# Expert inputs of a mixture-of-experts layer: selection matmuls replaced by rows gathered from DRAM

## The chip, the cores and the metric

The kernel runs on one core of one Trainium2 chip. The metric is the device time of one execution in microseconds, as the median of several runs. Traces come from one further execution under the hardware profiler.

## What is computed

One decoder layer on x of 512 tokens x 1024 features, float32. First three attention mixers in parallel, gated, projected and added; then a layer norm; then a mixture of experts with a second layer norm. The change lies in the mixture of experts:

```
x = layer_norm(ALPHA * x + mix)                    # x1: 512 x 1024
g = top-1 of 4 groups (softmax probability g_p)
two experts = top-2 of the 8 experts of that group
gate = g_p * softmax(the two logits)               # one weight per token and expert
for each expert e of 32, on the rows xb of x1 that chose it:
    h = silu(xb @ w_gate[e]) * (xb @ w_up[e])      # 1024 -> 512
    y = h @ w_down[e]                              # 512 -> 1024
out = layer_norm(ALPHA * x1 + sum over its two experts of gate * y)
```

There are 512 x 2 = 1024 assignments of a token to an expert. Each expert has three weight matrices of 2 MiB in float32, 192 MiB for all experts; each weight is read once.

## The kernel before

**Stages.** Up to about 411 us the attention part runs, with its weights streamed by SP through a pool of its own. From 411 to 450 us the last four blocks of the output projection are added to x1 tile by tile (project, in the order of the string ORDER, line 47), each tile of 128 tokens is normalised (norm, line 595), transposed (turn_x), routed (route) and ranked within its expert (rank). Then come 16 steps of two experts each, from 451 us on, and the second layer norm.

**Slots.** Each expert has 64 slots, so a pair of experts fills one tile of 128 rows. An assignment whose rank in its expert is 64 or more is left to an overflow loop (line 1138), which handles one expert with 64 further rows per iteration; how many iterations there are is known only on the chip (overflow_table, line 901, called in step 1; the count is read into a register of every engine at line 1137). The loop stands between step 7 and step 8 (MIDP = 7).

**One step** (pair_step, line 1016), in the order of TensorE, which is written out by hand: up(p, 0), the gate matrix, 16 matmuls of 64 slots x 512 columns, two experts side by side; the products of the step before are put back to token order and added to x1 for two token tiles (combine, line 789); up(p, 1), the up matrix; hidden (Silu on ScalarE, product on VectorE); combine of the other two tiles; selection for later pairs; turn (four transposes of the hidden rows, copied out as hT); info (per slot: its gate and its token number); down(p, 0) and down(p, 1). VectorE, ScalarE, GpSimd (Pool) and SP are ordered by the compiler's scheduler, each engine works its queue in order.

**Expert inputs.** An expert needs its rows of x1 transposed, 1024 features over partitions and slots in columns (xg). Before, this is a product with a 0/1 matrix: VectorE compares the slot numbers with each token's place (select; Quad.start, line 819, for two pairs at once, 256 columns), and TensorE multiplies x1 by it. Pair 0 does this while routing runs (gather0, line 870), pair 1 in float32 in step 0 (gather, line 744), and the pairs 2 to 15 by twos from a high and a low float32r half of x1 (split2 and Quad.gather, lines 808 and 828), 32 matmuls of 256 columns in a step, in steps 1 to 13. The two halves fill the tile xb, 32 KB a partition.

**Weights.** A weight matrix is fetched by SP in two pieces of 128 partitions x 2048 (1 MiB each, fetch, line 527). Pieces go round through 13 ring slots (RB, RA, RC, RD = 4, 5, 3, 1; lines 516 to 525); the tile xb holds four pieces before it is needed for x1's halves, and a tile named once holds two for step 0. A piece is issued when its slot's last reader on TensorE is done. ahead(n) (line 554) issues the next n pieces of the list; once the list of those fetched is used up, weights (line 540) issues one where it is asked for. Before the overflow loop as many pieces as the ring holds, less two, are issued (line 1133):

```
1130      with tc.manual_schedule(engines={mybir.EngineType.PE}):
1131          pairs[0].info()
1132          steps(range(MIDP + 1))
1133      ahead(RA + RB + RC + RD - 2)
```

At the loop's entry all engines meet, and SP waits until its DMAs have landed.

Of the kernel before, what the change touches and what calls it, by code (L numbers as in the profile page):

```python
# [22 lines left out]
P = 128  # L23
S = 512
# [12 lines left out]
RA, RB, RC, RD = 5, 4, 3, 1  # L37
HALF = 2048
MIDP = 7
# [11 lines left out]
def layer(ctx, tc, xT, xn, memT, w_qk, w_v, w_mk, w_mv, w_g, w_o, rb, oh, ln, wr, br,  # L51
# [562 lines left out]
    xbp = ctx.enter_context(pool("xb", waits="tile"))  # L614
# [6 lines left out]
    t = xbp.tile([P, 4 * HALF], F32, name="xb", tag="xb")  # L621
    ahead(4, [t[:, i * HALF:(i + 1) * HALF] for i in range(4)])
# [5 lines left out]
    i256 = rpool.tile([P, 256], F32, name="i256")  # L628
    ve.tensor_copy(i256[:, 0:P], i128)
    ve.tensor_scalar(out=i256[:, P:2 * P], in0=i128, scalar1=float(P), scalar2=None, op0=ALU.add)  # L630
# [90 lines left out]
    class Pair:  # L721
# [4 lines left out]
        def start(self):  # L726
            if self.p < 2:
                self.sel = gpool2.tile([P, TT, P], F32, name="sel", tag="sel", bufs=2)
                self.xg = (gpool2.tile([P, KT, P], F32, name="xg0", tag="xg0", bufs=1) if self.p == 0 else
                           quadp[0].tile([P, KT, 2 * P], F32, name="xg", tag="xg", bufs=2)[:, :, 0:P])  # L730
            else:
                self.sel = gpool2.tile([P, 2 * TT, P], BF16, name="sel", tag="sel", bufs=2)[:, 0:TT, :]
                self.xg = quads[self.p // 2].xg[:, :, self.p % 2 * P:self.p % 2 * P + P]
# [10 lines left out]
        def gather(self, c, bank="xgp"):  # L744
# [8 lines left out]
        def info(self):  # L753
            sp = bank3("ht" if self.p == 0 else "xgp")
            for t in range(TT):
                if self.p < 2:
                    pe.matmul(sp[:, 0:3], self.sel[:, t, :], gmx[:, t, self.p, :], start=t == 0, stop=t == TT - 1)
                else:
                    for i in range(3):
                        pe.matmul(sp[:, 0:3], self.sel[:, t, :], gmb[0][:, i, t, self.p, :], start=t + i == 0,  # L760
                                  stop=t + i == TT + 1)
            si = ep.tile([P, 8], F32, name="si", tag="si", bufs=3)
            ve.tensor_copy(si[:, 0:3], sp[:, 0:3])
            ve.tensor_copy(si[H[1], 0:1], sp[H[1], 1:2])
            self.si = si
# [40 lines left out]
    xb = [None]  # L806

    def split2(c):

        r = slice(c * 512, (c + 1) * 512)  # L810
        for t in range(TT):
            split(xb[0][:, 0, t, r], xb[0][:, 1, t, r], x1[:, t, r])

    class Quad:

        def __init__(self, m):
            self.m = m

        def start(self):
            self.sel = quadp[0].tile([P, TT, 2 * P], F32R, name="selq", tag="selq", bufs=1)  # L820
            self.xg = quadp[0].tile([P, KT, 2 * P], F32, name="xg", tag="xg", bufs=2)
            for t in range(TT):
                d = [d0[:, t, j, 2 * self.m:2 * self.m + 1] for j in range(2)]
                ve.tensor_scalar(out=self.sel[:, t, :], in0=i256, scalar1=d[0], scalar2=None, op0=ALU.is_equal)
                ve.scalar_tensor_tensor(out=self.sel[:, t, :], in0=i256, scalar=d[1], in1=self.sel[:, t, :].bitcast(F32),
                                        op0=ALU.is_equal, op1=ALU.add)

        def gather(self, i, bank):
            o = bank3(bank)
            for j in range(2):  # L830
                k = 2 * i + j
                for t in range(TT):
                    for part in range(2):
                        pe.matmul(o[:, j * 256:(j + 1) * 256], xb[0][:, part, t, k * P:(k + 1) * P], self.sel[:, t, :],  # L834
                                  start=t + part == 0, stop=t + part == TT)
            sc.copy(self.xg[:, 2 * i:2 * i + 2, :], o.rearrange("p (k t) -> p k t", t=256))  # L836

    quadp, quads = [], [Quad(m) for m in range(8)]

    def split_gates():  # L840
        gmb[0] = g = late[0].tile([P, 3, TT, 16, 3], BF16, name="gmb")
        f = lambda a: a.rearrange("p t a c -> p (t a c)")
        r = late[0].tile([P, TT * 48], F32, name="gr", tag="sq", bufs=1)
        ve.tensor_copy(f(g[:, 0]), f(gmx))
        ve.tensor_tensor(out=r, in0=f(gmx), in1=f(g[:, 0]), op=ALU.subtract)
        ve.tensor_copy(f(g[:, 1]), r)
        ve.tensor_tensor(out=f(g[:, 2]), in0=r, in1=f(g[:, 1]), op=ALU.subtract)
# [434 lines left out]
```

## Time and profile before

| | us |
|---|---|
| median of 3 runs | 961.93 |
| lowest, highest | 961.65, 962.98 |
| the profiled execution | 960.1 |
| its span, first to last instruction | 958.3 |

The page of the profile gives each engine's busy time in the span and, in 40 equal slices of 24 us, its busy share and what the DMA moved. The chain of waits follows the work that ended last back in time. A stretch is a window between two times of the span, with each engine's busy time, the granted clock of TensorE (1.00 is 2.4 GHz, 0.50 is 1.2 GHz), the share of the 16 DMA engines in use and GB/s. A timeline lists instructions in order; a DMA there is its issue, and its landing is told by its tile's view. PE is TensorE, PEld its weight load, DVE VectorE, ACT ScalarE, POOL GpSimd, SP the engine that issues most DMAs; a q behind an engine is its sequencer.

### The profile page before, as it was taken

How to read it: one execution, taken by the hardware profiler on the slowest of the kernel's cores; microseconds unless marked ns; L12 is line 12 of the kernel's file. 1: busy time of each engine (PE TensorE's matmuls, PEld its weight loads, DVE VectorE, ACT ScalarE, POOL GpSimd, SP SyncE). 2: the span in 40 equal slices, each digit the busy share in tenths (PEclk: the TensorE clock that was granted, in tenths of full speed). 3: DMA queues.
4: the chain of work that ended last, by engine and by line, in shares of the span. 5: the costliest groups of instructions: out<-in, count | busy, mean ns of one | idle time of the engine just before them, and what ended most of it. 6: DMA issues, size and time to landing. Idle time of an engine off the chain costs nothing.

```text
span 958.3 us, 12603 instructions
## 1 busy us (share of the span) xinstructions
PE 916.2 (96%) x4924; PEld 592.1 (62%) x4924; DVE 483.1 (50%) x1084; ACT 267.1 (28%) x505; POOL 30.7 (3%) x24
## 2 busy tenths in 40 slices
PE   7999999999999999999999999999879999999992
PEld 6888888787788888877554455445425455344430
DVE  5686776566764443478445353332234433332337
ACT  6365555456222222323131110011101111011013
POOL 2000000000000000310000000000000000000003
PEclk9999999999999999999999999999979999999997
DMA  8242231222344523378498999999989999999942
GB/s 301 75 134 89 93 118 63 82 73 67 134 178 140 197 88 102 101 313 346 176 369 334 415 421 421 420 419 421 420 319 374 421 420 421 421 421 420 420 180 88
DMA packets 44213, 249.52 MB, mean 260 GB/s; under 512 B 5713, under 2 KB 6904, under 8 KB 19704
## 3 DMA queue, kind: packets, MB, share of 16 engines
q1 hardware_dynamic: 42480, 247.84, 65.3%
q10 hardware_dynamic: 1672, 0.85, 0.4%
q8 instruction: 40, 0.66, 0.3%
q14 instruction: 21, 0.17, 0.1%
HBM read 246.57 MB, written 2.11 MB: 259 GB/s over the span
## 4 chain that ended last, share of the span: by engine, by line
PE 91%; DVE 5%; DMA 2%; ACT 1%; issue 1%; SPq 0%; POOL 0%; DVEq 0%; ACTq 0%; POOLq 0%
PE gu L982 23%; PE dn L1009 11%; PE pj L124 9%; PE pj L126 9%; PE pj L125 9%; PE xgp L834 3%; PE cb L834 3%; PE cb L798 2%; PE z L126 2%; PE z L124 2%; PE z L125 2%; PE y L278 2%; PE cb L799 2%; PE dn L798 1%; PE dn L799 1%; PE z L267 1%
## 5 line engine op out<-in xcount | busy, mean ns | idle before, releaser
L982 PE MATMUL gu<-r,xg 128*64 128x512 f32 x992 | 221.6, 600 | 8.8 <-DMA r<-in_we_dram 8.8
L982 PEld LDWEIGHTS gu<-r,xg 128*64 128x64 f32 x992 | 70.4, 138 | 148.3 <-issue 145.5
L103 DVE TENSOR_TENSOR wl<-wraw,wh 128x1024 fp32r<-128x1024 f32 (+2 forms) x71 | 82.3, 1162 | 86.1 <-ACT wh L102 85.7
L124 PE MATMUL pj<-xh,wh 128*128 128x512 f32 x304 | 120.7, 397 | 0.0
L125 PE MATMUL pj<-xh,wl 128*128 128x512 f32 x304 | 118.7, 390 | 1.1 <-DVE wl L103 1.1
L126 PE MATMUL pj<-xl,wh 128*128 128x512 f32 x304 | 118.9, 391 | 0.0
L1009 PE MATMUL dn<-r,hT 128*64 128x512 f32 x496 | 111.0, 596 | 1.2 <-ACT hT L999 1.2
L102 ACT CAST wh<-wraw 128x1024 fp32r<-128x1024 f32 (+2 forms) x71 | 70.3, 990 | 78.5 <-PE z L126 23.5
L801 DVE TENSOR_TENSOR x<-x,cb 128x512 f32<-128x512 f32 x60 | 38.4, 681 | 82.9 <-PE cb L799 78.6
L1009 PEld LDWEIGHTS dn<-r,hT 128*64 128x64 f32 x496 | 34.6, 137 | 64.3 <-issue 61.1
L124 PEld LDWEIGHTS pj<-xh,wh 128*128 128x128 f32 x304 | 57.1, 188 | 14.2 <-issue 2.0
L125 PEld LDWEIGHTS pj<-xh,wl 128*128 128x128 f32 x304 | 57.2, 188 | 12.7 <-DVE wl L103 1.4
L126 PEld LDWEIGHTS pj<-xl,wh 128*128 128x128 f32 x304 | 57.1, 188 | 12.0
L991 DVE SCALAR_TENSOR_TENSOR u<-gu,si,g 128x512 f32<-128x512 f32 x16 | 12.0, 750 | 99.1 <-PE gu L982 81.1
L836 ACT COPY xg<-xgp 128x512 f32<-128x512 f32 x14 | 8.2, 586 | 162.2 <-PE xgp L834 162.2
L103 DVE TENSOR_TENSOR y_l<-dn,y_h 128x512 fp32r<-128x512 f32 x31 | 21.4, 691 | 63.5 <-ACT y_h L102 63.3
L102 ACT CAST y_h<-dn 128x512 fp32r<-128x512 f32 x31 | 18.1, 585 | 94.5 <-PE dn L1009 94.5
L990 ACT ACTIVATE g<-gu 128x512 f32<-128x512 f32 x16 | 9.6, 598 | 108.6 <-PE gu L982 108.6
L385 ACT ACTIVATE gt<-pj 128x512 f32<-128x512 f32 x24 | 14.3, 598 | 89.9 <-PE pj L126 89.9
L801 DVE TENSOR_TENSOR x<-x,dn 128x512 f32<-128x512 f32 x60 | 38.3, 679 | 0.0
L834 PE MATMUL cb<-selq,xb 128*128 128x256 f32 x224 | 29.9, 286 | 0.0
L834 PEld LDWEIGHTS xgp<-selq,xb 128*128 128x128 f32 x224 | 28.6, 191 | 1.1
(626 smaller groups left out, 1390.0 us busy)
## 6 DMA issues: line engine op xcount, KB each, us to landing
r<-in_we_dram SPq DMA_DIRECT2D x185, 1024.0 KB, 11.5
wraw<-in_w_g_dram SPq DMA_DIRECT2D x32, 512.0 KB, 3.4
wraw<-in_w_qk_dram SPq DMA_DIRECT2D x14, 512.0 KB, 3.5
wraw<-in_w_v_dram SPq DMA_DIRECT2D x16, 384.0 KB, 3.5
wraw<-in_w_o_dram SPq DMA_DIRECT2D x8, 512.0 KB, 3.4
xb<-in_we_dram SPq DMA_DIRECT2D x4, 1024.0 KB, 7.1
xraw<-in_xT_dram SPq DMA_DIRECT2D x4, 512.0 KB, 6.4
x<-in_xn_dram SPq DMA_DIRECT2D x4, 512.0 KB, 5.5
```

The costliest lines, as they stand in the source:

```text
L102: sc.copy(dst_h, src)
L103: (gp if eng is gp else ve).tensor_tensor(out=dst_l, in0=src, in1=dst_h.bitcast(F32), op=ALU.subtract)
L124: pe.matmul(o, lh, rh, start=start and i == 0, stop=False)
L125: pe.matmul(o, ll, rh, start=False, stop=False)
L126: pe.matmul(o, lh, rl, start=False, stop=stop and i == n - 1)
L278: pe.matmul(ycur[0][H[a], i * P:(i + 1) * P], self.v[:, j, self.vcol + a * 64:self.vcol + a * 64 + 64], self.pT[a][:, j * P:(j + 1) * P], ...
L798: pe.matmul(o, sT, self.y_h[c][0:n], start=True, stop=False)
L799: pe.matmul(o, sT, self.y_l[c][0:n], start=False, stop=True)
L801: ve.tensor_tensor(out=x1[:, t, r], in0=x1[:, t, r], in1=o, op=ALU.add)
L834: pe.matmul(o[:, j * 256:(j + 1) * 256], xb[0][:, part, t, k * P:(k + 1) * P], self.sel[:, t, :], start=t + part == 0, stop=t + part == TT)
L982: pe.matmul(o[H[q]], pairs[p].xg[:, k, H[q]], held[q][:, k % 4 * 512:k % 4 * 512 + 512], start=k == 0, stop=k == KT - 1)
L1009: pe.matmul(o[H[q]], hT[:, k, H[q]], w[q][:, k * 512:(k + 1) * 512], start=k == 0, stop=k == 3)
```

## The change

Each tile of x1 is also stored to a DRAM tile xdr (512 x 1024) when it is normalised, by a DMA issued from Pool. For the pairs 1 to 15 the selection matmuls are gone, and with them Quad, xb, its split and the 256-column comparisons. Instead the slot information of pair p + 2 (its token numbers) is computed in step p between the two down products, turned into row numbers (rows), and Pool issues an indirect DMA that fetches up to 128 rows of 4 KB from xdr into one tile xrow; row numbers outside 0 to 511 (empty slots) are left out. In step p + 1, behind the combine, eight transposes make xg of it (spread). There is one xrow and one xg tile. Pair 1's information and rows are issued in step 0 behind up(0, 0). The information matmuls of a pair take the three bfloat16 parts of the gates in one product of nine columns, where there were three products. The freed space makes ring1 nine slots and ring3 four: 18 for 13. The overflow loop moves from behind step 7 to behind step 0 (overflow_table from step 1 to step 0), with six pieces issued ahead of it. The scaling of x1 by ALPHA moves from the end of step 0 to behind up(0, 0). The loop's body fetches its rows in the same way.

```diff
-RA, RB, RC, RD = 5, 4, 3, 1
+RA, RB, RC, RD = 9, 4, 4, 1
-MIDP = 7
+MIDP = 0
+BEFORE = 6
-    t = xbp.tile([P, 4 * HALF], F32, name="xb", tag="xb")
-    ahead(4, [t[:, i * HALF:(i + 1) * HALF] for i in range(4)])
     ahead(RA)
...
+        def info(self, bank="xgp"):
+            sp = bank3(bank)
+            si = ep.tile([P, 8], F32, name="si", tag="si", bufs=3)
+            if self.p < 2:
+                for t in range(TT):
+                    pe.matmul(sp[:, 0:3], self.sel[:, t, :], gmx[:, t, self.p, :], start=t == 0, stop=t == TT - 1)
+                ve.tensor_copy(si[:, 0:3], sp[:, 0:3])
+            else:
+                for t in range(TT):
+                    pe.matmul(sp[:, 0:9], self.sel[:, t, :], gmb[0][:, t * 16 + self.p, :], start=t == 0, stop=t == TT - 1)
+                ve.tensor_reduce(out=si[:, 0:3], in_=sp[:, 0:9].rearrange("p (i c) -> p c i", c=3), axis=AX.X, op=ALU.add)
...
+        def rows(self, n=P):
+
+            ix = ep.tile([P, 1], I32, name="ix", tag="ix", bufs=2)
+            ve.tensor_scalar(out=self.si[0:n, 3:4], in0=self.si[0:n, 2:3], scalar1=0.5, scalar2=BIG, op0=ALU.is_lt, op1=ALU.mult)
+            ve.scalar_tensor_tensor(out=ix[0:n], in0=self.si[0:n, 2:3], scalar=-1.0, in1=self.si[0:n, 3:4], op0=ALU.add, op1=ALU.add)
+            gp.indirect_dma_start(xrow[0][0:n], None, xdr, bass.IndirectOffsetOnAxis(ap=ix[0:n, 0:1], axis=0),
+                                  bounds_check=S - 1, oob_is_err=False)
+
+        def spread(self, c, bank):
+
             o = bank3(bank)
+            if c == 0:
+                self.xg = gpool2.tile([P, KT, P], F32, name="xg", tag="xg", bufs=1)
             for j in range(4):
                 k = 4 * c + j
-                srcs = [(x1[:, t, k * P:(k + 1) * P], self.sel[:, t, :]) for t in range(TT)]
-                for i, (a, b) in enumerate(srcs):
-                    pe.matmul(o[:, j * P:(j + 1) * P], a, b, start=i == 0, stop=i == len(srcs) - 1)
+                pe.transpose(o[:, j * P:(j + 1) * P], xrow[0][:, k * P:(k + 1) * P], ident)
             sc.copy(self.xg[:, 4 * c:4 * c + 4, :], o.rearrange("p (k t) -> p k t", t=P))
...
         if 1 in cols:
             norm(t, sm, lnb, op)
+            gp.dma_start(xdr[ts, :], x1[:, t, :])
...
-    quadp.append(ctx.enter_context(pool("quad", waits="tile")))
+    xrow[0] = ctx.enter_context(pool("rowp", waits="tile")).tile([P, D], F32, name="xrow")
+    gp.memset(xrow[0], 0.0)
...
         g = up(p, 0)
+        if p == 0:
+            pairs[1].info("cb")
+            pairs[1].rows()
+            pairs[0].info("ht")
+            for t in range(TT):
+                sc.mul(x1[:, t, :], x1[:, t, :], ALPHA)
...
-        for i, (of, u) in enumerate(units):
-            if i == n:
-                hT = turn(hs)
-            of.gather(u, ("xgp", "cb")[i % 2])
-        if p >= 14:
-            hT = turn(hs)
-        if p < 15:
-            pairs[p + 1].info()
-        for c in range(2):
-            down(p, hT, c)
+        if p < 15:
+            pairs[p + 1].spread(0, "xgp")
+        hT = turn(hs)
+        if p < 15:
+            pairs[p + 1].spread(1, "cb")
         if p == 0:
-            xb[0] = xbp.tile([P, 2, TT, D], F32R, name="xb", tag="xb")
-            split2(0)
-            split2(1)
-            for t in range(TT):
-                sc.mul(x1[:, t, :], x1[:, t, :], ALPHA)
-        if p == 1:
             overflow_table()
+        down(p, hT, 0)
+        if p < 14 and p != MIDP:
+            pairs[p + 2].info()
+            pairs[p + 2].rows()
+        down(p, hT, 1)
...
-            if p == 1 or p in range(2, 14, 2):
-                quads[p // 2 + 1].start()
-            if p + 1 < 16:
-                choose(p + 1)
+            if p + 2 < 16:
+                choose(p + 2)
             pair_step(p)
 
     with tc.manual_schedule(engines={mybir.EngineType.PE}):
-        pairs[0].info()
+        choose(1)
         steps(range(MIDP + 1))
-    ahead(RA + RB + RC + RD - 2)
+    ahead(BEFORE)
...
     with tc.manual_schedule(engines={mybir.EngineType.PE}):
         pairs[MIDP].places()
+        pairs[MIDP + 2].info()
+        pairs[MIDP + 2].rows()
         steps(range(MIDP + 1, 16))
```

## Rows read from the trace of the kernel before

**Rows 1.** The page: busy us (share of the span), and GB/s in 40 slices.
```profile
PE 916.2 (96%) x4924; PEld 592.1 (62%) x4924; DVE 483.1 (50%) x1084; ACT 267.1 (28%) x505; POOL 30.7 (3%) x24
GB/s 301 75 134 89 93 118 63 82 73 67 134 178 140 197 88 102 101 313 346 176 369 334 415 421 421 420 419 421 420 319 374 421 420 421 421 421 420 420 180 88
```

**Rows 2.** TensorE's waits, 440 to 960 us: total, times, longest, in us.
```profile
PE gu L982 <- DMA r<-in_we_dram: 8.8, 1, 8.8
```

**Rows 3.** The chain that ended last: start us, us, what.
```profile
602.82 6.87 PE gu L982 x32
...
622.68 0.44 PE ht L997 x4
...
632.34 6.87 PE gu L982 x32
...
880.24 6.87 PE gu L982 x32
...
906.46 6.87 PE gu L982 x32
```

**Rows 4.** Stretches: length, busy us by engine, clock, DMA share, GB/s.
```profile
448.00:456.00 8.00, 8.00 (x51) 4.62 (x51) 7.26 (x33) 1.17 (x2) 0.00 (x0) 1.00 0.56 169
466.00:482.00 16.00, 16.00 (x108) 10.30 (x109) 11.00 (x51) 6.57 (x13) 0.00 (x0) 1.00 0.07 14
506.00:512.00 6.00, 6.00 (x43) 2.52 (x43) 5.36 (x20) 1.17 (x2) 0.00 (x0) 1.00 0.32 97
696.00:732.00 36.00, 31.77 (x160) 14.82 (x162) 16.00 (x47) 2.84 (x5) 0.00 (x0) 0.87 0.83 320
```

**Rows 5.** The chain that ended last, at the overflow loop.
```profile
688.43 10.89 DMA r<-in_we_dram
```

**Rows 6.** Line 1138, the loop: durations ns, first and last start us.
```profile
L1138 PEldq EVENT_SEMAPHORE  x9: 51/51/51, 691.5 to 699.9; - x9
L1138 POOLq EVENT_SEMAPHORE  x8: 42/43/43, 694.4 to 699.8; - x8
```

**Rows 7.** A stretch of the loop; columns as in group 4.
```profile
696.00:700.00 4.00, 0.00 (x0) 0.00 (x0) 0.00 (x0) 0.00 (x0) 0.00 (x0) 0.50 0.34 135
```

**Rows 8.** A stretch at the kernel's start; columns PE, PEld, DVE, ACT, POOL.
```profile
10.00:20.00 10.00, 10.00 (x79) 10.00 (x79) 6.67 (x6) 7.31 (x11) 2.52 (x1) 1.00 1.02 384
```

**Rows 9.** The tile r, weight pieces: first and last start us; issue to landing.
```profile
L982 PE MATMUL gu<-r,xg x992: 592/593/1116, 450.9 to 921.8; 128*64 128x512 f32 x199
...
DMA to landing us min/median/max: 5.0/11.6/21.1
```

**Rows 10.** Timeline of SP, 411 to 467 us: first issue, length, pieces.
```profile
411.82 2.06 SPq L533 DMA_DIRECT2D xb<-in_we_dram  x4
413.92 21.54 SPq L533 DMA_DIRECT2D r<-in_we_dram  x8
440.52 0.80 SPq L533 DMA_DIRECT2D once<-in_we_dram  x2
450.06 8.79 SPq L533 DMA_DIRECT2D r<-in_we_dram  x5
```

**Rows 11.** Timeline of TensorE in step 0: start us, us, what.
```profile
464.82 3.84 PE L750 MATMUL xgp<-sel,x 128*128 128x128 f32 x32
...
476.88 3.60 PE L1009 MATMUL dn<-r,hT 128*64 128x512 f32 x16
```

**Rows 12.** Timeline of VectorE: the overflow table, from expert counts to iteration count.
```profile
514.09 0.19 DVE L912 COPY ov<-ht 128x32 f32<-128x32 f32 x1 [1.90 <-PE ht L910]
...
518.90 0.16 DVE L924 CAST ovi<-ove 1x17 int32<-1x17 f32 x1
```

**Rows 13.** Timeline of SP, 900 to 910 us: the last weight pieces.
```profile
903.05 4.24 SPq L533 DMA_DIRECT2D r<-in_we_dram  x4
```

**Rows 14.** DMA issues by size: KB each, median us to landing (the last two half pieces).
```profile
r<-in_we_dram SPq DMA_DIRECT2D x2, 512.0 KB, 12.4
```

**Rows 15.** Timeline of TensorE: the last down product.
```profile
931.31 3.65 PE L1009 MATMUL dn<-r,hT 128*64 128x512 f32 x14
```

More of the change, by code (lines that the diff above doesn't have):

```diff
@@ L613, in layer @@
     ring1 = ctx.enter_context(pool("ring1", bufs=RA, waits="tile"))
-    xbp = ctx.enter_context(pool("xb", waits="tile"))
     rpool = ctx.enter_context(pool("rout", waits="tile"))
@@ L742, in select @@
                                     op0=ALU.is_equal, op1=ALU.add)
-        def gather(self, c, bank="xgp"):
+        def info(self, bank="xgp"):
[9 more added lines that the diff above has]
+                ve.tensor_reduce(out=si[:, 0:3], in_=sp[:, 0:9].rearrange("p (i c) -> p c i", c=3), axis=AX.X, op=ALU.add)
+            ve.tensor_copy(si[H[1], 0:1], si[H[1], 1:2])
+            self.si = si
@@ L751, in gather @@
             sc.copy(self.xg[:, 4 * c:4 * c + 4, :], o.rearrange("p (k t) -> p k t", t=P))
-        def info(self):
-            sp = bank3("ht" if self.p == 0 else "xgp")
-            for t in range(TT):
[L756 to L765, printed above, removed]
@@ L804, in combine @@
                                                 op1=ALU.add, accum_out=sums[:, t, c:c + 1])
[L806 to L836, printed above, removed]
@@ L838, in layer @@
-    quadp, quads = [], [Quad(m) for m in range(8)]
-    def split_gates():
[L841 to L847, printed above, removed]
+    def split_gates():
+        gmb[0] = g = late[0].tile([P, TT * 16, 9], BF16, name="gmb")
+        f = lambda a: a.rearrange("p t a c -> p (t a) c")
+        r = late[0].tile([P, TT * 16, 3], F32, name="gr", tag="sq", bufs=1)
+        ve.tensor_copy(g[:, :, 0:3], f(gmx))
+        ve.tensor_tensor(out=r, in0=f(gmx), in1=g[:, :, 0:3], op=ALU.subtract)
+        ve.tensor_copy(g[:, :, 3:6], r)
+        ve.tensor_tensor(out=g[:, :, 6:9], in0=r, in1=g[:, :, 3:6], op=ALU.subtract)
@@ L849, in layer @@
+    xdr = ctx.enter_context(pool("xdrp", space=DRAM)).tile([S, D], F32, name="xdr")
+    xrow = [None]
     late, gmb = [None], [None]
@@ L895, in layer @@
         settle()
+    pairs[0].xg = gpool2.tile([P, KT, P], F32, name="xg", tag="xg", bufs=1)
     for c in range(2):
@@ L1030, in pair_step @@
             pairs[p - 1].combine((3,), banks=("dn", "dn"))
-        units = []
-        if p == 0:
-            units = [(pairs[1], 0), (pairs[1], 1)]
-        elif p < 14:
-            units = [(quads[p // 2 + 1], i) for i in (range(4) if p == 1 else range(2) if p % 2 == 0 else range(2, 4))]
-        n = (len(units) + 1) // 2
-        for i, (of, u) in enumerate(units):
-            if i == n:
-                hT = turn(hs)
-            of.gather(u, ("xgp", "cb")[i % 2])
-        if p >= 14:
-            hT = turn(hs)
-        if p < 15:
-            pairs[p + 1].info()
-        for c in range(2):
-            down(p, hT, c)
-        if p == 0:
-            xb[0] = xbp.tile([P, 2, TT, D], F32R, name="xb", tag="xb")
-            split2(0)
-            split2(1)
-            for t in range(TT):
-                sc.mul(x1[:, t, :], x1[:, t, :], ALPHA)
-        if p == 1:
-            overflow_table()
+        if p < 15:
[3 more added lines that the diff above has]
+            pairs[p + 1].spread(1, "cb")
+        if p == 0:
+            overflow_table()
+        down(p, hT, 0)
[3 more added lines that the diff above has]
+        down(p, hT, 1)
         if p != MIDP:
@@ L1141, in layer @@
         sel = gpool2.tile([P, 2, TT, 64], F32, name="sel_o", tag="sel", bufs=2)
-        selb = quadp[0].tile([P, TT, 64], F32R, name="selb_o", tag="selq", bufs=1)
         for t in range(TT):
@@ L1146, in layer @@
                                  op0=ALU.is_equal)
-        ve.tensor_tensor(out=selb, in0=sel[:, 0], in1=sel[:, 1], op=ALU.add)
         ve.tensor_scalar(out=dv, in0=dv, scalar1=-64.0, scalar2=None, op0=ALU.add)
@@ L1155, in layer @@
         ve.tensor_copy(pair.si[0:64, 2:3], sp[0:64, 1:2])
-        pair.xg = gpool2.tile([P, KT, P], F32, name="xg0", tag="xg0", bufs=1)
+        pair.rows(64)
+        pair.xg = late[0].tile([P, KT, 64], F32, name="xg_o")
         o = bank3("xgp")
         for k in range(KT):
-            for t in range(TT):
-                for j in range(2):
-                    pe.matmul(o[:, k * 64:(k + 1) * 64], xb[0][:, j, t, k * P:(k + 1) * P], selb[:, t, :],
-                              start=t + j == 0, stop=t + j == TT)
+            pe.transpose(o[:, k * 64:(k + 1) * 64], xrow[0][0:64, k * P:(k + 1) * P], ident[0:64, 0:64])
         sc.copy(pair.xg[:, :, 0:64], o.rearrange("p (k t) -> p k t", t=64))
```

6 lines of the change are left out of this document (removed).

## The prediction

> **What bounds the kernel now.** I read the page's busy shares and slices first, then what TensorE waited for, then the chain of waits, then rates by stretch.
>
> TensorE is busy for 916.2 of 958.3 us, but from slice 23 on the DMA moves 420 GB/s in nearly every slice as well [rows 1]. So the expert stage (its first matmul on a weight piece is at 450.9 us [rows 9]) has two candidates at once. TensorE waited for a weight exactly once, 8.8 us, at the overflow loop [rows 2]; otherwise it sets the pace. One step of two experts takes 632.34 - 602.82 = 29.52 us with the selection matmuls in it, and 906.46 - 880.24 = 26.22 us in step 14, which has none [rows 3]. The weights of a step are 12 pieces of 1 MiB = 12.58 MB; at 421 GB/s a piece takes 2.49 us and a step's weights 29.9 us. The two limits are therefore 0.4 us apart: whatever is taken off TensorE's step is worth nothing by itself, because the weight stream is next. What counts is when that stream ends, and how long after it the kernel does.
>
> When the stream stood still is read from stretches under 421 GB/s [rows 4]. Loss = length x (1 - rate/421): 448 to 456 us, 4.8; 466 to 482, 15.5; 506 to 512, 4.6; 696 to 732 (overflow loop), 8.6. The first three are a full ring; the fourth is the loop. At its entry SP waits until every weight in flight has landed, 10.89 us from 688.43 [rows 5]. TensorE reaches the loop's semaphores at 691.5 and stands there; Pool comes at 694.4; TensorE leaves the last one at 699.9, 0.6 us behind the last landing [rows 6]. Over 696 to 700 the clock stands at 0.50, that is 1.2 GHz, after about 4 us without matmuls [rows 7].
>
> **The change part by part.**
>
> *Step without selection matmuls.* Removed: the Quad selections on VectorE and their matmuls. Added: 8 transposes a step; four cost 0.44 us [rows 3], so 0.88. The step becomes 26.22 + 0.88 = 27.1 us (the three-term information sum goes from 12 small matmuls to 4; 0.2 us, not counted). The two copies of 128x512 out of PSUM stay as they were. Gain on TensorE: 2.4 us a step, but see the stream.
>
> *Rows from DRAM.* The overflow loop's body leaves no row in the trace of before, so it ran no iteration and all 2 x 512 assignments sit in the 64-row slots: 1024 rows over 16 pairs, on average 64 valid rows of 4 KB a pair = 0.262 MB, the others dropped by the bounds test. No gather stands in the trace. Nearest row for 4 KB rows: at 10 to 20 us, when 512 KB loads over 128 partitions run, the DMA is full at 384 GB/s [rows 8]. So 0.68 us a gather, and for the 14 gathers behind the loop 9.6 us of the stream. It can't be below 14 x 0.262 MB / 421 GB/s = 8.7, since the same DMA engines must move the bytes. Upper end: all 128 rows are fetched, 19.1 us. I take 9.6, because rows of that size are what the nearer row moved.
>
> Weighed against a page: the trace shows a lone 1 MiB weight landing 5.0 us after its issue [rows 9], though in the stream one lands every 2.49; the 2.5 us of start and completion are overlapped there. The Trainium skill's "DMA: Bandwidth & Descriptors", section "Anatomy of one DMA — SWDGE (gpsimd) path", gives a DMA that GpSimd issues a constant of about 2.0 us plus bytes over 436 GB/s. If that constant were taken from the stream at each gather, 14 of them would cost an estimated 36 us instead of 9.6. The trace's overlapped 2.5 us speaks against it, but for SP's queue only.
>
> *Storing x to DRAM:* four 512 KB stores as each row tile is normalised, before 451 us, 2.1 MB / 384 = 5.5 us of DMA. They push the prefetch back, into the 4.8 us hole at 448 to 456 [rows 4]; experts 0 and 1 have their first weights long before. Pool issues them between the four norms' powers; nothing else is queued on Pool there. ScalarE's scaling of x by alpha (four operations, moved to behind the first up) now waits for the last store, and queued behind it on ScalarE is the first Silu, wanted by the first hidden row at 466. I put it at nothing, since the last store follows the last norm by one landing, 5 us; if it came 10 us late, TensorE's step 0 would be a few us longer and the restart below with it.
>
> *Slots.* The 9 slots that hold x's split and ring1 before become 9 of ring1, and ring3 has 4 for 3: 18 instead of 13 slots that return. Before, 4 + 4 + 8 + 2 + 5 = 23 pieces had been issued by 467 us [rows 10], and the next waited until 480.5 for down(0). After: 20 are fetched ahead and 6 more go to the slots of pieces 0 to 5, which up(0) frees by 463 (the last two in the middle of up(0, 1)). Before, the 23 had landed by 467, where the rate falls to nothing [rows 4]; the 26 land by 467 + 3 x 2.5 + 5.5 (stores) - 4.8 (the hole they fill) + 0.7 (first gather) = 476 us.
>
> *The loop after step 0.* Step 0 ended at 480.5 (476.88 + 3.60) [rows 11]. It loses the two selection units, 3.84 us the first [rows 11], 7.2 net of their overlap, and gains 0.9 for transposes, 0.2 for the overflow count and about 1.2 because the copy of hT is no longer covered: 475.6. The first gather is on the path here: its information matmul follows up(0, 0), which starts at 450.9 [rows 9] and takes 7 [rows 3], so 458.5; VectorE, Pool and the DMA follow, and it is wanted behind up(0, 1), at 466.5. Eight us against 5.0 for a lone 1 MiB [rows 9]; I allow 3.4 us late in the bad case, 479. The overflow table moves here too: VectorE's part to the iteration count took 514.09 to 519.06 [rows 12], 5.0 us; beginning at about 469 it is ready by 474 and its tail of as many small operations by 479. All engines came to the loop's semaphores within 2.9 us of TensorE, and left 0.6 after the last landing [rows 6]: SP issues again between 475.6 + 3.5 = 479 and 484 (gather late, or the table's tail last). I take 482 against 480.5 before (+1.5). TensorE's stop, and a slow clock behind it, cost only TensorE, which has 14 landed pieces in hand.
>
> *After that the stream does not stop.* 18 slots hold 14 pieces at the restart, 4 are issued at once (10 us), and up(1) frees two each 3.5 us. Weights and gather need 29.9 + 0.68 = 30.6 us a step, TensorE 27.1: it eats 1.4 pieces of its lead a step, and waits for weights from about step 9. By itself it would end down(15) at 482 + 15 x 27.1 + 3 (slow clock) = 891.5.
>
> **The sum.** Last weights are issued up to 907.29 [rows 13], the half pieces land 12.4 us after issue [rows 14]; with the last issued at about 906.9 that is 919.3. Changes to that: no stop at 506 to 512, -4.6; no loop at step 7, -8.6; 26 instead of 23 pieces landed at the restart, -7.5; 14 gathers, +9.6; restart, +1.5. Total -9.6: the last weight lands at 909.7, later than the 891.5, so the stream binds. Now the tail: before, down(15)'s last matmul ended at 934.96 [rows 15] and the span 23.3 us later. TensorE lagged the last weight by 15.7 us; after, it has only the last half piece to do, half of 3.65, 1.8 us. Span: 909.7 + 1.8 + 23.3 = 934.8 us. The profiled execution took 960.1 with a span of 958.3, so 936.6; the median of the runs is 1.8 above the profiled one: **938.5 us**, 2.4% faster. LayerNorm's parameters (1 MiB, 2.5 us) come behind the last weight and are wanted only when the last sums are done, behind the last matmul: covered.
>
> **The rivals.**
> 1. *Rows dearer than their valid bytes* (all 128 fetched, or a gather at half rate): +9.5, so 948 us. For: no gather was seen. Against: the diff gives a bounds test that drops rows. Chance 0.13.
> 2. *The gather stops the stream* (other side). Place: steps 1 to 14, each gather holds the DMA engines for its whole issue to landing time: 5.0 - 2.49 + 0.68 = 3.2 us instead of 0.68, 14 x 2.5 = +35: 974 us. It decides from 2.35 us a gather ((961.9 - 938.5) / 14 = 1.67 over the 0.68). For: a second queue in a saturated stream is untested here. Against: a stream of SP's own DMAs overlaps the same latency. By the constant of the Trainium skill's page named above it would be an estimated 965. Chance 0.07, a mild form of it (within 0.2% of before) 0.03.
> 3. *TensorE's clock falls while it waits for weights.* Price: a step at 1.2 GHz takes about twice 27.1, so some 20 us over the stream's 30.6 in each of six steps, over 1050 us. For: the 0.50 at the loop [rows 7]. Against: waits of 3.5 us a step are split over six pairs of pieces, 0.6 us each, while 0.50 came after 4 us in one. Chance 0.03.
> 4. *TensorE stays the bound* (the change doesn't turn the kernel to the stream): by its own 891.5 + 23.3 + 3.6 = 918 us. It needs 166 pieces in less than 410 us from 482, while 166 x 2.49 = 413, and the gathers come on top; only a faster stream would allow it. Chance 0.02.
>
> **How the numbers follow.** Forecast 0.72, its own range 933 (restart at 479, gathers at 8.7, the tail 2 us shorter) to 944 (restart at 484, the hole of 4.8 not filled). Rival 1 stretches it to 951. Low 931, high 953 hold about 0.87 by this account; the rest of the unseen gather lies outside. A measurement of this kernel can tell about 0.2% (2 us) from no change. Faster: 0.72 + 0.13 + 0.02 = 0.87; same 0.03; slower 0.07 + 0.03 = 0.10.
>
> **What would show it.** Right: rows "TensorE waits for DMA r" of some tenths of a us, dozens of them, from about step 9 on; the DMA at 415 to 421 GB/s from 485 to 912 without a hole; the last weight landing at 910 and the span's end 25 us behind it; gathers landing within 20 us of issue, before their transposes. Wrong: the rate under 400 GB/s in the middle (rival 2, or 1), a wait of TensorE for xrow in each step, a clock of 0.5 in the last third (rival 3), or a hole behind the new loop longer than 5 us.

## The result

The changed kernel takes 948.16 us (median of 4 runs, 944.51 to 948.60) against 961.79 us for the kernel before on the same chip (960.39 to 962.98): a ratio of 0.985, 95% interval 0.9823 to 0.9878. That is 13.6 us faster. The forecast was 23.4 us faster, at 938.5 us; the time lies inside the range, 9.7 us above the point. The profiled execution took 944.51 us with a span of 942.7 us.

The page: busy us (share of the span), GB/s in 40 slices, and the queue that carries GpSimd's DMAs (packets, MB, share of the 16 engines). They answer to [rows 1].

```profile
PE 885.9 (94%) x4420; PEld 544.5 (58%) x4420; DVE 458.3 (49%) x1048; ACT 261.6 (28%) x497; POOL 50.3 (5%) x44
...
GB/s 297 86 122 103 78 135 68 67 68 68 138 178 145 198 90 90 111 326 384 384 201 394 421 420 421 419 420 420 420 420 420 419 420 420 421 420 421 420 301 89
...
q0 software_dynamic: 2736, 6.11, 1.7%
```

TensorE lost 30 us of work (916.2 to 885.9). The two slices under 400 GB/s at the old loop (319 and 374) are gone; one slice of 201 is left, at the new one.

TensorE's waits from 440 to 960 us (total, times, longest), which answer to [rows 2]:

```profile
PEld gu L954 <- DMA r<-in_we_dram: 28.1, 26, 2.8
...
PE gu L954 <- DMA r<-in_we_dram: 11.7, 9, 1.9
...
PE xgp L765 <- DMA xrow<-xdr,ix: 3.4, 1, 3.4
PE xgp L745 <- DVEq L1102: 2.2, 1, 2.2
```

One wait for a weight, at the loop, has become nine small ones of the matmuls and 26 of the weight loads (PEld), whose waits partly run beside matmuls. Before, the weight loads waited eight times, 2.5 us in all, which the row in [rows 2] does not show. Which of the two limits sets the pace is seen in the chain that ended last (start us, us, what; answers to [rows 3]):

```profile
566.13 6.87 PE gu L954 x32
...
593.18 6.87 PE gu L954 x32
...
620.22 6.87 PE gu L954 x32
...
627.74 19.82 DMA r<-in_we_dram
...
688.75 20.50 DMA r<-in_we_dram
...
872.72 20.48 DMA r<-in_we_dram
893.24 3.65 PE gu L954 x14
...
898.93 7.90 PE gu L954 x32
...
910.04 3.68 PE dn L981 x16
...
915.84 3.58 PE dn L981 x14
```

Up to 620 us the chain runs through TensorE, one step in 620.22 - 593.18 = 27.04 us. From 627.74 us on it runs through weights, each 19.8 to 21.0 us from issue to landing. TensorE's matmuls wait for a weight from 688 us on, in step 8, and from 734 us on a step takes 30.6 us ((886.96 - 733.86) / 5, the starts of its gate products).

The same stretches as in [rows 4], the long middle, and SyncE's first issue behind the loop (length, busy us by engine, clock, DMA share, GB/s; then start us, length, pieces):

```profile
448.00:456.00 8.00, 8.00 (x54) 4.74 (x54) 3.77 (x22) 5.51 (x7) 0.00 (x0) 1.00 0.87 328
466.00:482.00 16.00, 11.18 (x54) 5.09 (x50) 9.49 (x69) 2.93 (x5) 0.00 (x0) 0.89 0.39 160
506.00:512.00 6.00, 6.00 (x34) 2.02 (x32) 2.96 (x14) 0.59 (x1) 0.99 (x1) 1.00 0.99 373
696.00:732.00 36.00, 34.07 (x156) 13.62 (x158) 11.56 (x33) 4.44 (x9) 0.99 (x1) 1.00 1.01 419
484.00:900.00 416.00, 399.57 (x1832) 163.78 (x1830) 139.56 (x347) 47.28 (x85) 13.82 (x14) 1.00 1.01 418
```

```profile
482.66 2.24 SPq L534 DMA_DIRECT2D r<-in_we_dram  x4
```

The stream now runs at 418 GB/s from 484 to 900 us. What is left is the stop behind step 0: by 473 us the pieces issued ahead have landed, and the next is issued at 482.66.

### The profile page after: what moved, and what is told of

It is laid out like the page before. It is cut to its first block, busy times and chain, and to the rows that moved or that the text cites. A ratio compares the mean times of both kernels' runs of the same rounds, so it can differ in the third digit from the quotient of the medians.

```text
span 942.7 us, 11649 instructions
## 1 busy us (share of the span) xinstructions
PE 885.9 (94%) x4420; PEld 544.5 (58%) x4420; DVE 458.3 (49%) x1048; ACT 261.6 (28%) x497; POOL 50.3 (5%) x44
## 5 line engine op out<-in xcount | busy, mean ns | idle before, releaser
L954 PE MATMUL gu<-r,xg 128*64 128x512 f32 x1008 | 240.2, 600 | 11.7 <-DMA r<-in_we_dram 11.7
L954 PEld LDWEIGHTS gu<-r,xg 128*64 128x64 f32 x1008 | 76.9, 137 | 162.4 <-issue 134.2
L981 PE MATMUL dn<-r,hT 128*64 128x512 f32 x512 | 117.4, 598 | 5.5 <-ACT hT L971 5.5
L127 PEld LDWEIGHTS pj<-xl,wh 128*128 128x128 f32 x304 | 57.1, 188 | 12.1
L755 POOL DMA_INDIRECT xrow<-xdr,ix x15 | 14.9, 994 | 399.2 <-DVE sel L732 319.5
L104 POOL TENSOR_TENSOR wol<-wraw,woh 128x1024 fp32r<-128x1024 f32 x4 | 10.9, 2754 | 327.4 <-ACT woh L103 327.4
```

The costliest lines, as they stand in the source:

```text
L104: (gp if eng is gp else ve).tensor_tensor(out=dst_l, in0=src, in1=dst_h.bitcast(F32), op=ALU.subtract)
L127: pe.matmul(o, lh, rl, start=False, stop=stop and i == n - 1)
L755: gp.indirect_dma_start(xrow[0][0:n], None, xdr, bass.IndirectOffsetOnAxis(ap=ix[0:n, 0:1], axis=0), bounds_check=S - 1, oob_is_err=False)
L954: pe.matmul(o[H[q]], pairs[p].xg[:, k, H[q]], held[q][:, k % 4 * 512:k % 4 * 512 + 512], start=k == 0, stop=k == KT - 1)
L981: pe.matmul(o[H[q]], hT[:, k, H[q]], w[q][:, k * 512:(k + 1) * 512], start=k == 0, stop=k == 3)
```

## The experiments

The table holds all kernels. "Stop ends" is the first weight issued behind the stop at step 0, "last weight" its landing, both in the profiled execution, in us from the span's start; the ratio is to the kernel before, run beside it. The changed kernel has two runs, whose ratios differ by 0.0026, 2.5 us; differences below are against after0, and against the first run each gain is 2.5 us smaller.

| kernel | stop ends | last weight | span | median us | ratio (95% interval) |
|---|---|---|---|---|---|
| before | 480.5 | 919.8 | 958.3 | 961.8 | 1 |
| changed, first run | 482.7 | 913.1 | 942.7 | 948.2 | 0.985 (0.9823 to 0.9878) |
| after0 | 488.5 | 917.6 | 947.2 | 949.0 | 0.9876 (0.9857 to 0.9895) |
| nogather | 487.3 | 905.6 | 935.0 | 938.0 | 0.977 (0.975 to 0.979) |
| allrows | 490.7 | 927.7 | 956.5 | 957.6 | 0.9946 (0.993 to 0.9963) |
| loop7 | 483.6 | 916.9 | 951.8 | 952.6 | 0.9898 (0.9872 to 0.9924) |
| slots13 | 483.5 | 926.8 | 956.4 | 960.3 | 1.0002 (0.999 to 1.0013) |
| quarter | 482.3 | 914.4 | 944.0 | 945.6 | 0.9837 (0.9816 to 0.9858) |
| before8 | see there | 915.3 | 944.9 | 947.2 | 0.9879 (0.9856 to 0.9903) |
| early | 485.1 | 915.5 | 945.2 | 942.4 | 0.9811 (0.9796 to 0.9827) |
| mullate | 483.4 | 912.7 | 942.3 | 944.1 | 0.9833 (0.9817 to 0.9849) |
| noloop | 482.8 | 911.5 | 941.0 | 942.9 | 0.9814 (0.9789 to 0.9839) |
| bothfixes | 482.0 | 911.0 | 940.6 | 941.9 | 0.9805 (0.9779 to 0.9832) |
| loopend | 473.4 | 901.9 | 932.4 | 935.8 | 0.9741 (0.9728 to 0.9755) |

Two regularities hold it together. With the changed kernel's gathers, its 18 slots and six pieces issued ahead of a loop behind step 0, the last weight lands 429 to 430.5 us after the stop ends (917.6 - 488.5, 913.1 - 482.7, 915.5 - 485.1, 912.7 - 483.4, 911.0 - 482.0). And in all of them but the kernel before (38.5), allrows (28.8), loop7 (34.9) and loopend (30.5) the span ends 29.4 to 29.7 us behind the last weight. So a delay of the stop is paid at the end, all but a us or so.

**after0** is the changed kernel again, without an edit.

> The changed kernel itself, again. Theory (the weight stream sets the end): in every execution the span ends about 460.0 us after SP's first issue behind the loop (942.7 - 482.7 in the profiled one), so executions of 948 us have that issue at about 486, because TensorE's clock fell at 470 us while it waited for the first gather and stayed low through step 0's down products. Rival: the 3.6 us between executions come from the end or from the gathers; then the issue stays at 482 to 483. Time 944 to 949 us.

It measured 949.0 us. Its stop ended at 488.5 instead of 482.7, and its span is 4.5 us longer; it ends 458.7 us behind that issue, so the theory holds there. Its reason does not: the wait for the rows (3.9 us for 3.4) explains only a little, and step 0's first matmul on a weight already starts at 455.3 instead of 451.2. The clock fell once more, earlier, in the routing stage (columns as above):

```profile
443.00:450.00 7.00, 7.00 (x41) 6.88 (x39) 4.84 (x41) 1.17 (x2) 0.00 (x0) 0.51 1.00 375
```

In the first run's trace that stretch has clock 1.00. That trace is of the fastest of the four executions: its mean granted clock is 0.988, that of the other three 0.983 to 0.984. So part of the miss sits in front of the part that the prediction worked on; "mullate" below takes it up.

**The gathers' price: nogather and allrows.** The first drops two calls:

```
             pairs[p + 2].info()
-            pairs[p + 2].rows()
...
         pairs[MIDP + 2].info()
-        pairs[MIDP + 2].rows()
```

> The changed kernel without the 14 row gathers of pairs 2 to 15: the indirect DMA and its two small VectorE operations are left out, the transposes read the rows of pair 1 again, so the experts' inputs from pair 2 on are not the reference's. Everything else stays, the transposes too. Theory: the gathers take 14 x 0.70 us from a stream that sets the end, so 9.8 us less than the changed kernel, 938 us. Rival a (TensorE or the gather's latency sets the end, the stream is not touched): 948 us, no change. Rival b (a gather holds the stream for issue to landing, 3.2 us): the stream would end 45 us earlier and TensorE's own pace of 27.1 us a step would bind, about 920 us.

The second lets empty slots pass the bounds test, with row 0:

```
-  scalar1=0.5, scalar2=BIG, op0=ALU.is_lt, op1=ALU.mult
+  scalar1=0.5, scalar2=1.0, op0=ALU.is_lt, op1=ALU.mult
```

> The changed kernel with empty slots fetching row 0 instead of being left out, so that every gather moves 128 rows (0.52 MB); their gate is zero, so nothing of the output depends on them. Theory: empty slots are left out in the changed kernel, and bytes are what a gather costs: 14 x 0.24 MB more at 384 GB/s = +9 us, 957 us. Rival a (empty slots were fetched or cost a packet's time anyway): 948 us. Rival b (a gather costs a fixed time, whatever its bytes): 948 to 950 us.

Without gathers the time falls by 0.0106 of 961.4, 10.2 us, 0.73 us a gather; from stop to last weight it is 418.3 instead of 429.1 us, 0.77 a gather. The queue of GpSimd's DMAs from 484 to 905 us in after0, then in allrows (packets, MB, share of the 16 engines):

```profile
q0 software_dynamic: 2016, 3.81, 2.4%
```

```profile
q0 software_dynamic: 2016, 7.34, 4.4%
```

3.81 MB over 14 gathers is 0.272 MB, 66 rows of 4 KB; 2.4% of 421 us is 10.1 us, 0.72 a gather. With all 128 rows it is 0.524 MB and 4.4%, 18.5 us. allrows took 957.6 us, as its theory said, and from stop to last weight 437.0 us, 18.7 more than nogather. So nearly all of the price goes with the bytes, the empty slots move none, and the latency (8.3 us from issue to landing, below) is not charged to the stream. Rival 2 of the prediction falls. So does rival 1, although its 948 us is the time that was measured: the rows cost what their valid bytes do, and the missing 10 us lie elsewhere, as the next section shows. By the Trainium skill's "DMA: Bandwidth & Descriptors", section "Anatomy of one DMA — SWDGE (gpsimd) path", a constant of about 2.0 us belongs to each DMA. The runs show that a saturated stream does not pay it: 0.72 to 0.77 us a gather.

**What the loop's place is worth: loop7.** `MIDP = 7` and 16 pieces ahead of it; the rest is the changed kernel.

> The changed kernel with the overflow loop back behind step 7 and 16 pieces issued ahead of it (two less than the ring holds, as before). Theory: a stop of the stream costs its length wherever it stands, and behind step 0 the ring is full anyway: the hole of 11 us there shrinks to about 5 and a hole of 6 to 9 us opens at the loop, so 945 to 951 us, the same as the changed kernel. Rival (the gain came from taking TensorE's stop and slow clock, 12 us, out of the middle): 958 to 962 us.

952.6 us, 0.0022 of 961 or 2 us above after0 (the intervals overlap), a little above the theory's range and well under the rival's. The hole behind step 0 shrank to 4.4 us (479.2 to 483.6), as expected. TensorE now stands far longer at the loop than before the change, first its one long wait there, then the stretch (columns as above):

```profile
PE xgp L745 <- issue: 31.5, 1, 31.5
```

```profile
680.00:716.00 36.00, 8.03 (x30) 2.58 (x32) 4.87 (x22) 0.00 (x0) 0.98 (x1) 0.54 0.91 363
```

With 18 slots and 16 pieces ahead there is more in flight for the loop's entry to wait for, while the DMA still moves 363 GB/s; that reading was not tested further. Taking the loop out of the middle is thus worth 2 us by the ratios and 4 by the medians, not clear of noise, and not 8.6.

**What the slots are worth: slots13.**

```
-RA, RB, RC, RD = 9, 4, 4, 1
+RA, RB, RC, RD = 5, 4, 3, 1        # and the list of pieces in the order of the kernel before
```

> The changed kernel with the ring of the kernel before: 13 slots instead of 18 (five, four, three and one), and the list of pieces reordered for them as before; the gathers, the small matrices and the overflow loop behind step 0 stay. Theory (the slots buy the restart): 21 instead of 26 pieces have landed when SyncE starts again behind the loop, 5 pieces at 2.49 us is 12.4 us, and the holes ahead of the loop come back (some 4 us at 448 to 456): 960 to 966 us, which is the time of the kernel before, so that the gain of the change would hang on the slots alone. Rival (the slots do not matter, because the weights only become the bound later): within 2 us of the changed kernel's 949.

960.3 us, the time of the kernel before to 0.0002. Five slots are worth 0.0126 of 960, 12.1 us; five pieces at 2.49 us are 12.45. The last weight lands 443.3 us after the stop instead of 430: the same five pieces. Without the slots the change would have bought nothing.

**What TensorE's relief alone is worth: quarter**, made from the kernel before.

```
-  for t in range(TT):        # in Quad.gather
+  for t in range(1):
...                           # stop= to match
```

> The kernel before with one of the four token tiles in its selection matrices (a quarter of their matrix multiplications; the inputs of the experts are those of that tile alone), everything else as it was: 13 slots, no gather, the loop in the middle. TensorE's step goes from 29.5 to 26.7 us. Theory (the two limits stand 0.4 us a step apart, so that TensorE's relief only buys its lag behind the last weight): the last weight lands at 916 to 920 us as before, TensorE's last matrix ends some 6 us behind it instead of 15.7, 949 to 953 us. Rival A (TensorE is the bound and the stream follows it): 14 steps by 2.8 us less, 39 us, 926 us. Rival B (the stream alone): 960 to 962.

945.6 us, 15.7 us faster than before: more than the theory gave (949 to 953) and far less than rival A (926). TensorE follows the last weight by 29.6 us to the end of the span instead of 38.5: that is 8.9, near the 9.7 expected. But the last weight is also 5.4 us earlier, which fits a TensorE that frees the 13 slots sooner. Two stretches of [rows 4] in quarter, and the one ahead of the second, before and in quarter:

```profile
506.00:512.00 6.00, 6.00 (x34) 1.94 (x30) 3.69 (x15) 1.17 (x2) 0.00 (x0) 1.00 1.01 408
696.00:732.00 36.00, 34.80 (x162) 13.94 (x164) 16.61 (x48) 3.33 (x6) 0.00 (x0) 0.91 0.93 371
```

```profile
675.00:696.00 21.00, 16.42 (x102) 9.12 (x98) 5.00 (x10) 2.83 (x5) 0.00 (x0) 0.98 1.01 419
```

```profile
675.00:696.00 21.00, 0.00 (x0) 0.00 (x0) 0.00 (x0) 0.00 (x0) 0.00 (x0) 0.50 0.91 378
```

408 for 97 GB/s is worth 6 x 311 / 421 = 4.4 us. The loop is reached earlier in quarter, so its loss is counted from 675 to 732 us: 8.7 us before, 2.1 + 4.3 = 6.4 in quarter, 2.3 less. A stop at step 0 that ends 1.8 us later takes some of it back; that makes 4.9 of the 5.4.

**Three edits at the stop: before8, early, mullate.** before8: `BEFORE = 8`.

> The changed kernel with 8 instead of 6 pieces issued ahead of the overflow loop. Theory (the stream is the bound from there to its end, so that a hole in it is paid in full): the hole at the loop, 10 to 11 us in the changed kernel, closes by two pieces of 2.49 us; the loop is reached at most 1 us later; 944 to 946 us. Rival A (the slots for the two pieces come free only as step 0 ends, so that SyncE reaches the loop later by as much): 948 to 950. Rival B (the end of the run is set by TensorE): 948 to 950, with a last weight that lands 4 us earlier and a TensorE that does not follow it.

Nothing gained (0.9879 against 0.9876), which is rival A. The seventh and eighth piece get a slot only at 480 us, and the loop's entry then waits for their landing; TensorE's wait there, and the two stretches around it:

```profile
PE xgp L745 <- DMA r<-in_we_dram: 5.2, 1, 5.2
```

```profile
474.00:482.00 8.00, 7.40 (x44) 3.51 (x46) 5.50 (x46) 2.15 (x4) 0.00 (x0) 1.00 0.39 118
482.00:490.00 8.00, 2.83 (x16) 0.92 (x14) 2.70 (x13) 0.58 (x1) 0.00 (x0) 0.75 0.63 247
```

early:

```
+        if p == 0:
+            pairs[1].info("cb")
+            pairs[1].rows()
         g = up(p, 0)
         if p == 0:
-            pairs[1].info("cb")
-            pairs[1].rows()
             pairs[0].info("ht")
+            choose(2)                  # taken out of steps()
```

> The changed kernel with the first gather ahead of the first up matrix of step 0 instead of behind it, and the choice for pair 2 (VectorE) behind the lists of pairs 0 and 1. Theory (the wait of 3.4 us for the first gather, and the half clock after it, move the restart behind the loop and with it the whole stream): no wait for the row tile in step 0, clock 1.00 there, restart 4 to 7 us earlier, 942 to 945 us. Rival (the piece order or the loop itself sets the restart): restart and time as in the changed kernel, 948 to 949.

942.4 us, 0.0065 or 6.3 us better than after0. No wait for the row tile is left among TensorE's waits, and the clock stays at 1.00 from 466 to 482 us. The trace is not of a median execution, though: it is the slowest of seven, 946.98 us, its stop ends 3.5 us earlier than in after0, and its clock is 0.57 from 443 to 450 us. Five executions took 941.1 to 942.8 us at a mean granted clock of 0.988 to 0.991, the other two 946.5 and 947.0 at 0.983 and 0.982. That suggests that five escaped the fall at 443 us, so that the 6.3 us hold two gains: some 2 us from the earlier gather (946.5 to 947.0 against 949.0), the rest from the fall that did not come. None of the five has a trace, so this is not shown.

mullate: the factor is read from a tile that hangs on step 0's first list.

```
+            al = ep.tile([P, 1], F32, name="al")
+            ve.tensor_scalar(out=al, in0=pairs[0].si[:, 0:1], scalar1=0.0, scalar2=ALPHA, ...)
...
-                sc.mul(x1[:, t, :], x1[:, t, :], ALPHA)
+                sc.mul(x1[:, t, :], x1[:, t, :], al)
```

> The changed kernel with the four multiplications by ALPHA on ScalarE (1.04 us each) held behind step 0's first list: their factor is read from a tile that is worked out from that list. In the changed kernel the first stands ahead of a copy of the routing stage for which TensorE waits (1.4 us), and in most executions the granted clock then falls to half for 7 us at 443 us. Theory (this wait, not the stores on GpSimd, lets the clock fall): the wait is 0.6 us or less, as in the kernel before, clock 1.00 from 425 to 455, restart behind the loop some 4 us earlier, 944 to 946 us. Rival (the stores to DRAM delay the norm, or the fall is there whatever ScalarE does): the half clock stays, 948 to 949.

944.1 us, 0.0043 or 4.1 us better than after0, and its executions lie within 2.0 us (943.12 to 945.13), those of the changed kernel's two runs within 5.3 (944.51 to 949.82). The one execution of the changed kernel whose trace is without the fall took 944.51. ScalarE's rows in after0 show what was moved (start us, us, what):

```profile
439.02 0.19 ACT L601 ACTIVATION_READ_ACCUMULATOR sq<-x,sm 128x1 f32 x1
439.11 1.04 ACT L996 ACTIVATE x<-x 128x1024 f32<-128x1024 f32 x1
440.06 1.05 ACT L649 COPY xt<-gu 128x512 f32<-128x512 f32 x2
```

The same place, and the clock, in mullate:

```profile
439.20 1.07 ACT L649 COPY xt<-gu 128x512 f32<-128x512 f32 x2
```

```profile
443.00:450.00 7.00, 6.29 (x60) 6.20 (x61) 6.32 (x51) 3.28 (x4) 0.00 (x0) 1.00 0.99 371
```

Of the nine kernels' traces with the multiplication in front of that copy, seven have a clock of 0.50 to 0.57 in this stretch (all but the first run and slots13); of the five without it, the kernel before among them, none has. So the fall came only with the multiplication there, and not when it was held back. Why two traces escaped is not shown: TensorE's wait for that copy is 1.1 us in them as well, against 0.3 in mullate.

**The loop itself: noloop, bothfixes, loopend.** noloop drops the loop's lines.

> The changed kernel without the overflow loop (neither its entry nor its body; the data of this case never enter the body). In the changed kernel SyncE issues nothing for 11 us before it leaves the loop, and the stream is dry as long. Theory (the loop, which SyncE may pass only with all engines, holds it): the next pieces are issued as slots come free, from about 478 to 480 us, the hole is 3 to 4 us instead of 10 to 11, and the 2.2 us that TensorE waits at the loop go too: 940 to 942 us. Rival (the slots hold it: all 18 are full until step 0 has used them): the hole only moves, as with 8 pieces ahead of the loop; 945 to 948.

942.9 us, 6 us better than after0 (3.5 better than the first run): near the theory. The hole is 4.3 us (478.6 to 482.8) instead of 10.7. The stretch behind step 0 in after0, then in noloop:

```profile
476.00:490.00 14.00, 11.77 (x56) 5.00 (x56) 7.34 (x54) 2.93 (x5) 0.00 (x0) 0.83 0.07 17
```

```profile
476.00:490.00 14.00, 13.75 (x70) 6.49 (x72) 9.86 (x67) 2.92 (x5) 1.00 (x1) 0.88 0.50 187
```

bothfixes is early and mullate together.

> The changed kernel with both repairs: the first gather ahead of step 0's first up matrix, and the four multiplications on ScalarE held behind the first list. Alone they gave 6.3 and 4.1 us. Theory (two stalls of different stages that both move the restart, and the half clock at 443 us spoils some of the first repair's executions): the gains add up at least in part, 937 to 941 us, with clock 1.00 from 425 us to the loop. Rival (they are the same gain, the stream being late once): 942 to 944.

941.9 us, no better than early alone within the intervals. The two gains did not add up. If most executions of early had already escaped the half clock, as their clocks suggest, most of mullate's gain was in early's 6.3 us.

loopend is bothfixes with the loop moved from behind step 0 to behind step 15 (the lines of the two repairs are left out):

```
-        steps(range(MIDP + 1))
-    ahead(BEFORE)
+        steps(range(16))
     ovi, dv = over
     ...                                # the loop, unchanged
-    with tc.manual_schedule(engines={mybir.EngineType.PE}):
-        pairs[MIDP].places()
-        pairs[MIDP + 2].info()
-        pairs[MIDP + 2].rows()
-        steps(range(MIDP + 1, 16))
+    pairs[15].places()
```

> The changed kernel with both repairs and the overflow loop moved once more, from behind step 0 to behind step 15, where no weight is left to fetch; pair 15's scatter matrix is made behind it. Theory (in the changed kernel a slot comes back 3.6 us before step 0 ends, in the middle of its down product, and the loop's entry takes 2.2 us more, so that the loop holds the stream for 5.8 us): the hole of the stream around 480 us shrinks by that, the last weight lands at 905 to 906 us instead of 911; behind it the loop's entry costs 2 to 4 us of the tail, which is now 32 to 34 us instead of 29.6. Together 938 to 940 us against 941.9 for the two repairs alone. Rival (the hole is the slots' alone, or the loop costs as much at the end as it did behind step 0): last weight 909 to 911, 943 to 946 us.

935.8 us, ratio 0.9741: 25 us faster than the kernel before and the fastest of all. The stretches 466 to 482 and 476 to 490 in bothfixes, then in loopend, and TensorE's one wait at loopend's loop:

```profile
466.00:482.00 16.00, 13.35 (x73) 4.94 (x68) 9.46 (x69) 5.07 (x8) 0.00 (x0) 1.00 0.63 260
476.00:490.00 14.00, 11.92 (x58) 4.09 (x55) 8.67 (x51) 1.77 (x3) 1.00 (x1) 1.00 0.52 193
```

```profile
466.00:482.00 16.00, 15.42 (x84) 5.78 (x80) 11.70 (x83) 2.83 (x5) 1.00 (x1) 1.00 0.90 358
...
476.00:490.00 14.00, 14.00 (x66) 5.30 (x64) 5.67 (x23) 1.18 (x2) 1.00 (x1) 1.00 1.01 425
```

```profile
PE cb L798 <- DVE sT L772: 2.2, 1, 2.2
```

SyncE's first issue is at 473.41, right behind the first half of the down product, which runs from 469.73 for 3.65 us: a slot comes back there, half a product and the loop's 2.1 us (TensorE's wait there in bothfixes) earlier than behind the loop (476.99, where the product ends, + 2.1 - 473.41 = 5.7, as expected). The last weight is 9.0 us earlier than in bothfixes; the other 3 us are a step 0 that began that much earlier in this execution (down product at 469.73 against 472.74). The tail pays little: 30.5 us behind the last weight instead of 29.6, 0.9 where 2 to 4 were expected.

## Why the prediction was right and wrong

**Right: the stream becomes the bound.** It is shown by the chain, by 418 GB/s from 484 to 900 us, and by spans that follow the last weight. The step of 27.1 us measured 27.04. With the waits a step took 30.6, as forecast, and they began in step 8, for its "about step 9". The clock held at 1.00 through the waits, so rival 3 did not come; nor did rival 4, since TensorE waits for weights from 688 us on.

**Right: the gathers.** Charged at 0.68 us, they measured 0.72 to 0.77: 10.1 to 10.75 us for the forecast's 9.6. Rivals 1 and 2 are out, though the 948 us of rival 1 came: that is a coincidence of the three misses below. Each landed long before its transposes, except the first. Over all gathers of the changed kernel, GpSimd's issue (busy us, mean ns; idle before it) and the landing:

```profile
L755 POOL DMA_INDIRECT xrow<-xdr,ix x15 | 14.9, 994 | 399.2 <-DVE sel L732 319.5
```

```profile
DMA to landing us min/median/max: 7.5/8.3/8.6
```

**Right in place: the stop behind step 0.** Forecast 482, measured 482.66 in the profiled execution, which is the fastest; in after0, whose trace is of a median execution, it is 488.5. The first gather was 3.4 us late, the bad case of the forecast to the tenth; that was an allowance and not a sum, so the tenth is luck. A stop longer than 5 us was named as a sign of error, and it is there: the 26 pieces had landed by 473, not 476, so 9 to 10 us passed without a weight.

**Wrong by 4.5 us: the tail.** The forecast let down(15) end 1.8 us behind the last weight. It ended at 919.42, 6.3 us behind 913.1; the 23.3 us from there to the span's end were right. The step that failed was "it has only the last half piece to do". The last up piece lands at 903.1 and its group ends at 906.83 (898.93 + 7.90); behind it TensorE has the scatter of pair 14, the transposes, the wait for the hT copy and two halves of the down product with the first half's scatter between them, 12.6 us in all, while the four pieces that follow land within 10. The last piece but four sets the end, not the last.

**Wrong by 3.4 us: the last weight.** 913.1 against 909.7. The stop ended 0.7 us late, and from there the weights took 430.4 us instead of 427.7. Of these 2.7 the gathers are 0.5 to 1.2. About 1.2 more is a slow start that the forecast left out when it booked the stop at 506 to 512 us as gone: the stream moved 382 GB/s from 500 to 506 us and 373 from 506 to 512. And 0.5 lies in the base: the kernel before's last weight landed at 919.8, where the sum took 919.3 from the median landing of the two half pieces. 934.8 + 4.5 + 3.4 = 942.7, the measured span.

**Wrong by 1.8 us: the executions.** The median was put 1.8 us above the profiled execution, as in the kernel before; it is 3.65 above. The step that failed was that ScalarE's scaling "now waits for the last store" and costs nothing. It does not wait for that store: in the first run's trace the first of its four operations runs at 437.95 us, and the last store is issued at 441.18. It stands in the routing stage ahead of a copy on TensorE's path, where the clock then fell in most traces. mullate, which holds it back, takes 944.1 us, 4.1 under after0 (against the first run the intervals overlap).

**Terms whose sum held and whose sizes did not.** "No loop at step 7, -8.6" was the loss there in the kernel before; undone alone (loop7) the move is worth 2 to 4 us, not clear of noise, and the loop still costs some 6 behind step 0 (noloop). Against that, the slots were credited with 7.5 us and carry 12.1. And "whatever is taken off TensorE's step is worth nothing by itself" was wrong as a sentence: quarter gained 15.7 us, 8.9 of the lag that the forecast booked under the tail, and 5.4 of a last weight that lands sooner. The balance, if the parts add up, is: relief worth 15.7 by itself; gathers -10.2; slots +12.1; and -5.7 that is left over, as slots13 gained nothing. It would go with step 0, its first gather and its loop, but was not measured by itself.

## What to carry to other kernels

Where two limits stand within a few tenths of a us per step, count the time of the saturated stream: its bytes, its stops, and what still has to run behind its last pieces, of which the last that heads a long chain counts, not the last to land. A loop that every engine must pass belongs where nothing is left to fetch. An operation moved "to a later place" in the text can move earlier on its engine once the thing that held it back is gone; look at what is queued behind it there.

## What was not expected of the hardware

A gather by GpSimd of 66 rows of 4 KB takes 0.72 to 0.77 us from a stream that runs at 420 GB/s, while it lands 8.3 us after its issue and occupies GpSimd for 0.99 us; dropped rows move no bytes (3.81 against 7.34 MB, 2.4% against 4.4% of the 16 engines). And one operation of 1.04 us in front of a copy was enough for the granted clock to stand at about half for 7 us in seven of nine traces; step 0 then began some 4 us later (455.3 for 451.2), and the rest with it.
